# Loading the first tile of a row-maximum kernel by two DMAs, one of 16 partitions and one of 112

## The chip, the cores and the metric

One Trainium2 chip, one core of it. The metric is the device time of a run in microseconds (us). Engines that matter: DVE (VectorE) reduces, SP (SyncE) issues the loads, and 16 DMA engines move the data from HBM into SBUF, the on-chip memory of 128 partitions. Where a number below is called a landing, it is the time from the start of the profiled span to the semaphore event that tells that a DMA is complete.

## The reference

```python
x = np.random.randn(8192, 8192).astype(np.float32)
return np.linalg.norm(x, ord=np.inf, axis=1)      # the largest |x| of each row
```

256 MiB are read once; 32 KB are written.

## The kernel before

48 of the 64 rows that each partition gets are read as 24 bulk tiles, each 128 partitions x 16384 floats (64 KB in each partition, two rows of the input). One `reduce_max` handles a tile. The remaining rows (the tail) are read in smaller and smaller pieces. Three buffers take turns.

```python
x_b = x[:split].rearrange("(a p n b) c -> a n p (b c)", p=P, a=A, n=G, b=B)
...
sbuf = ctx.enter_context(tc.tile_pool(name="sbuf", bufs=BUFS))      # BUFS = 3
...
for a in range(A):
    for n in range(G):
        t = sbuf.tile([P, B * cols + 16], F32, tag="t")
        nc.sync.dma_start(out=t[:, : B * cols], in_=x_b[a, n])
        absmax(r_bulk[:, a, n * B : (n + 1) * B],
               t[:, : B * cols].rearrange("p (b c) -> p b c", b=B))
...                                   # the tail, stores
nc.at_finalize(start_first_load_early)   # moves the first load ahead of the opening barrier
```

Consecutive partitions read addresses 256 KB apart (`n * b * c` floats), and every partition's share of a tile is one contiguous 64 KB run.

Of the kernel before, what the change touches and what calls it, by code (L numbers as in the profile page):

```python
# [1 line left out]
logging.getLogger("concourse").setLevel(logging.ERROR)  # L3

# [1 line left out]

# [4 lines left out]

F32 = mybir.dt.float32
X = mybir.AxisListType.X



TAIL = (
    [[8192]] * 8
    + [[4096, 4096]] * 5
    + [[2048] * 4] * 2  # L20
    + [[2048, 2048, 2048, 1024, 512, 512]]
)


def start_first_load_early(nc):


    sp = mybir.EngineType.SP
    first, *rest = nc.main_func.blocks
    for block in rest:  # L30
        insts = block.instructions
        for i, ins in enumerate(insts):
            if ins.engine == sp and type(ins).__name__ == "InstDMACopy":
                assert not ins.sync_info.on_wait
                moved = insts[i]
                block.instructions = insts[:i] + insts[i + 1 :]
                head = first.instructions
                at = next(k for k, h in enumerate(head) if h.engine == sp)
                first.instructions = head[:at] + [moved] + head[at:]
                return  # L40


@with_exitstack
def kernel(
    ctx: ExitStack,
    tc: tile.TileContext,
    x: bass.AP,
    out: bass.AP,
    G: int = 4,
    B: int = 2,  # L50
    BUFS: int = 3,
):
    nc = tc.nc
    P = nc.NUM_PARTITIONS
    rows, cols = x.shape


    n_tail = len(TAIL)
    assert n_tail % B == 0
    n_bulk_rows = rows // P - n_tail  # L60
    assert n_bulk_rows % (G * B) == 0
    A = n_bulk_rows // (G * B)
    split = n_bulk_rows * P
    x_b = x[:split].rearrange("(a p n b) c -> a n p (b c)", p=P, a=A, n=G, b=B)
    out_b = out[:split].rearrange("(a p n b) -> p a (n b)", p=P, a=A, n=G, b=B)
    x_t = x[split:].rearrange("(p t b) c -> t p (b c)", p=P, b=B)
    out_t = out[split:].rearrange("(p t) -> p t", p=P)

    sbuf = ctx.enter_context(tc.tile_pool(name="sbuf", bufs=BUFS))
    outp = ctx.enter_context(tc.tile_pool(name="outp", bufs=1))  # L70

    k_last = len(TAIL[-1])
    r_bulk = outp.tile([P, A, G * B], F32)
    r_tail = outp.tile([P, n_tail], F32)
    r_fin = outp.tile([P, 1], F32)
    k_max = max(len(r) for r in TAIL[:-1])
    part = outp.tile([P, n_tail - 1, k_max], F32)
    nc.vector.memset(part[:], 0.0)  # L78

    def absmax(o, i):  # L80
        nc.vector.reduce_max(out=o, in_=i, axis=X, apply_absolute_value=True)  # L81

    for a in range(A):
        for n in range(G):
            t = sbuf.tile([P, B * cols + 16], F32, tag="t")
            nc.sync.dma_start(out=t[:, : B * cols], in_=x_b[a, n])
            absmax(
                r_bulk[:, a, n * B : (n + 1) * B],
                t[:, : B * cols].rearrange("p (b c) -> p b c", b=B),
            )  # L90
    nc.scalar.dma_start(out=out_b, in_=r_bulk[:])

    for i in range(0, n_tail, B):
        t = sbuf.tile([P, B * cols + 16], F32, tag="t")
        for j in range(B):
            r = i + j
            at = j * cols
            last = r == n_tail - 1
            for k, w in enumerate(TAIL[r]):
                nc.sync.dma_start(  # L100
                    out=t[:, at : at + w], in_=x_t[i // B][:, at : at + w]
                )
                if last and k == k_last - 1:

                    absmax(r_tail[:, : n_tail - 1], part[:])
                    nc.scalar.dma_start(
                        out=out_t[:, : n_tail - 1], in_=r_tail[:, : n_tail - 1]
                    )
                    absmax(r_fin[:], t[:, at : B * cols + k_last - 1])
                elif last:  # L110
                    absmax(
                        t[:, B * cols + k : B * cols + k + 1], t[:, at : at + w]
                    )
                else:
                    absmax(part[:, r, k : k + 1], t[:, at : at + w])
                at += w
    nc.sync.dma_start(out=out_t[:, n_tail - 1 :], in_=r_fin[:])
    nc.at_finalize(start_first_load_early)


# [1 line left out]
_INS = ['x']  # L122
_OUTS = [((8192,), 'float32')]


# [23 lines left out]
```

## Time and profile before

| | before |
|---|---|
| time, median of 6 runs | 629.2 us |
| span of the profiled run | 627.3 us |
| DMA queue q1, share of 16 engines' time | 99.2% |
| DVE busy | 552.7 us, 88% |
| first bulk reduction starts | 22.03 us |
| distance between later bulk reductions | 19.3 to 19.4 us |

The page of the kernel before: busy times, DMA rate in 40 slices of the span, the load queue, the chain that ended last, and the group of bulk reductions (its last columns are the engine's idle time before them and what ended it).

```profile
DVE 552.7 (88%) x58; POOL 0.2 (0%) x4
GB/s 401 468 401 464 405 460 410 455 414 451 418 451 418 451 418 447 422 447 422 447 422 447 422 447 422 447 422 443 426 420 428 425 433 435 426 429 427 427 425 274
q1 hardware_dynamic: 8208, 268.44, 99.2%
DMA 64%; DVE 30%; another core or an unknown queue 4%; issue 1%; SPq 0%
L81 DVE TENSOR_REDUCE r_bulk<-t 128x2 f32<-128x16384 f32 x24 | 413.3, 17220 | 69.7 <-DMA t<-in_x_dram 69.7
```

The load queue is the limit: it is busy from end to end, while the DVE waits 69.7 us in all before its bulk tiles. The alternation of 401 and 468 in the rate is only that packets are booked at their start: in a finer view of the same trace (its first 23 us in 40 slices) single slices of 0.575 us swing between 0 and 1254 GB/s while the queue is 96.7% busy.

The timeline of the kernel before, its first three bulk reductions (start, duration, engine, line, operation, shapes, and in brackets the idle time before and what ended it):

```profile
22.03 17.22 DVE L81 TENSOR_REDUCE r_bulk<-t 128x2 f32<-128x16384 f32 x1 [21.05 <-DMA t<-in_x_dram]
41.32 17.22 DVE L81 TENSOR_REDUCE r_bulk<-t 128x2 f32<-128x16384 f32 x1 [2.07 <-DMA t<-in_x_dram]
60.67 17.22 DVE L81 TENSOR_REDUCE r_bulk<-t 128x2 f32<-128x16384 f32 x1 [2.14 <-DMA t<-in_x_dram]
```

A reduction takes 17.22 us, a tile's load 19.3 us, so each reduction starts when its tile lands. One level down are the DMA packet records of the trace. Each 64 KB run is one packet. On every one of the 16 engines the packets follow each other without a gap at 2.418 us each (65,536 bytes in 2.418 us are 27.1 GB/s). Eight of them make a tile: 19.34 us.

### The profile page before, as it was taken

How to read it: one execution, taken by the hardware profiler on the slowest of the kernel's cores; microseconds unless marked ns; L12 is line 12 of the kernel's file. 1: busy time of each engine (PE TensorE's matmuls, PEld its weight loads, DVE VectorE, ACT ScalarE, POOL GpSimd, SP SyncE). 2: the span in 40 equal slices, each digit the busy share in tenths (PEclk: the TensorE clock that was granted, in tenths of full speed). 3: DMA queues.
4: the chain of work that ended last, by engine and by line, in shares of the span. 5: the costliest groups of instructions: out<-in, count | busy, mean ns of one | idle time of the engine just before them, and what ended most of it. 6: DMA issues, size and time to landing. Idle time of an engine off the chain costs nothing.

```text
span 627.3 us, 196 instructions
## 1 busy us (share of the span) xinstructions
DVE 552.7 (88%) x58; POOL 0.2 (0%) x4
## 2 busy tenths in 40 slices
DVE  0588988889988889888898888998889999999998
POOL 0000000000000000000000000000000000000000
DMA  9999999999999999999999999999999999999996
GB/s 401 468 401 464 405 460 410 455 414 451 418 451 418 451 418 447 422 447 422 447 422 447 422 447 422 447 422 443 426 420 428 425 433 435 426 429 427 427 425 274
DMA packets 9138, 268.49 MB, mean 428 GB/s; under 512 B 1968, under 2 KB 1968, under 8 KB 2352
## 3 DMA queue, kind: packets, MB, share of 16 engines
q1 hardware_dynamic: 8208, 268.44, 99.2%
q10 hardware_dynamic: 928, 0.03, 0.1%
q14 instruction: 2, 0.02, 0.0%
HBM read 268.44 MB, written 0.03 MB: 428 GB/s over the span
## 4 chain that ended last, share of the span: by engine, by line
DMA 64%; DVE 30%; another core or an unknown queue 4%; issue 1%; SPq 0%
DMA t<-in_x_dram 64%; DVE r_bulk L81 24%; DVE part L81 5%; DVE t L81 1%; SPq L100 0%; DVE r_fin L81 0%
## 5 line engine op out<-in xcount | busy, mean ns | idle before, releaser
L81 DVE TENSOR_REDUCE r_bulk<-t 128x2 f32<-128x16384 f32 x24 | 413.3, 17220 | 69.7 <-DMA t<-in_x_dram 69.7
L81 DVE TENSOR_REDUCE part<-t 128x1 f32<-128x4096 f32 (+2 forms) x26 | 130.0, 5067 | 1.3 <-DMA t<-in_x_dram 1.3
L81 DVE TENSOR_REDUCE t<-t 128x1 f32<-128x2048 f32 (+2 forms) x5 | 8.6, 1746 | 0.3 <-DMA t<-in_x_dram 0.3
L78 DVE MEMSET part<- 128x60 f32 x1 | 0.1, 108 | 0.9 <-PEq L133 0.9
L81 DVE TENSOR_REDUCE r_fin<-t 128x1 f32<-128x517 f32 x1 | 0.7, 691 | 0.0
L81 DVE TENSOR_REDUCE r_tail<-part 128x15 f32<-128x60 f32 x1 | 0.2, 216 | 0.0
L133 POOL MEMSET const-bfloat16-1.0<- 128x1 bf16 x1 | 0.1, 101 | 0.0
L133 POOL MEMSET const-uint8-127<- 128x1 uint8 x1 | 0.1, 101 | 0.0
L133 POOL MEMSET const-float32-0.0<- 128x1 f32 x1 | 0.1, 98 | 0.2 <-issue 0.2
L133 POOL MEMSET const-float32-1.0<- 128x1 f32 x1 | 0.1, 98 | 0.0
## 6 DMA issues: line engine op xcount, KB each, us to landing
t<-in_x_dram SPq DMA_DIRECT2D x8, 4096.0 KB, 37.0
t<-in_x_dram SPq DMA_DIRECT2D x10, 2048.0 KB, 30.4
t<-in_x_dram SPq DMA_DIRECT2D x11, 1024.0 KB, 24.6
t<-in_x_dram SPq DMA_DIRECT2D x1, 512.0 KB, 15.9
t<-in_x_dram SPq DMA_DIRECT2D x2, 256.0 KB, 13.2
t<-in_x_dram SPq DMA_DIRECT2D x24, 40.7
out_dram<-r_bulk ACTq DMA_DIRECT2D x1, 24.0 KB, 57.9
out_dram<-r_tail ACTq DMA_DIRECT2D x1, 7.5 KB, 5.6
```

What stands on the lines that cost most here:

```text
L78: nc.vector.memset(part[:], 0.0)
L81: nc.vector.reduce_max(out=o, in_=i, axis=X, apply_absolute_value=True)
L133: nc = _bacc.Bacc("TRN2", target_bir_lowering=False, num_devices=1)
```

## The change

The first tile is loaded in two parts. The first has 16 partitions, so that each DMA engine has only one descriptor (one contiguous run, one 64 KB packet in the trace); this part is the load that is moved ahead of the opening barrier. The intent is to have all 16 engines at work sooner.

```diff
-            nc.sync.dma_start(out=t[:, : B * cols], in_=x_b[a, n])
+            for lo, hi in ((0, 16), (16, P)) if a == n == 0 else ((0, P),):
+                nc.sync.dma_start(
+                    out=t[lo:hi, : B * cols], in_=x_b[a, n][lo:hi, :]
+                )
```

## The prediction

> **What bounds the kernel now.** The load stream. On the page, queue q1 holds its 16 DMA engines 99.2% of the span and moves 268.44 MB; the DVE is busy 88% and before nearly every bulk reduction it waits about 2.1 us for a DMA (chain of waits, timeline). The trace's packet records show each bulk row as one 65,536-byte packet of 2.418 us, back to back on each of 16 engines (27.1 GB/s each), so a tile of 128 rows costs 8 x 2.418 = 19.34 us, which is the distance between landings (22.00, 41.29, 60.65 us). The DVE needs 17.22 us per tile, so it never sets the pace. The end is start-up, 256 packet times on the engine that lags most, and a tail of about 5 us.
>
> **What the change hopes for.** The first load is issued at 0, its sequencer time is 0.38 us, and the 16 engines take their first packet between 1.02 and 2.05 us; second packets start between 3.89 and 4.75 us. One row per engine should hand all engines work at about 1.0 us. The second part is issued right after the opening barrier (about 0.79 us) and should be queued before a first packet ends. If rows always took 2.418 us, the lagging engine would gain at most 4.75 - 3.89 = 0.86 us; I would say 0.7 us: 628.5 us. The extra issue (0.33 us on SP) is off the path; semaphores shift by one, but every wait keeps its place (instruction orders compared).
>
> **What I think it costs.** Which partitions an engine writes changes. [...] Every load of this trace covers 128 partitions, so it shows nothing of this. [...] The other 112 rows are 7 per engine. [...]the queue has no slack, so nothing is won back. [...]
>
> **On the critical path:** all of it; it delays the first landing from 22.0 to about 38 us and everything after equally.
>
> **Prediction:** 644 us, range 628 to 648. Faster by over 2%: 1%; within 2%: 43%; slower by over 2%: 56%.
>
> **What would show it.** [...] First reduction starting at 36 to 39 us; later landings again 19.34 us apart; the DMA rate low in the page's first slices only; DVE busy time unchanged at 552.7 us.
>
> [...]

The sum came to 644 us: the 629.2 us of the kernel before and about 15 us more, the first landing moving from 22.0 to about 38 us.

## The result

| | before | after |
|---|---|---|
| time, median of 6 runs | 629.2 us (629.04 to 629.8) | 650.55 us (650.19 to 651.07) |
| ratio, 95% interval | | 1.0338 (1.0324 to 1.0351) |
| first landing (both parts) | 22.00 us | 43.32 us |
| DVE busy | 552.7 us | 552.7 us |

The change makes the kernel 21.35 us slower. The ratio is the mean time of the changed kernel's fast runs over that of the other's fast runs of the same rounds, so it is not quite the ratio of the medians.

The same lines of the page, after:

```profile
DVE 552.7 (85%) x58; POOL 0.2 (0%) x4
GB/s 194 251 319 404 441 453 437 412 445 449 404 441 453 429 412 453 445 404 445 449 416 429 453 441 408 445 449 404 441 424 437 431 427 437 419 434 433 422 425 251
q1 hardware_dynamic: 8224, 268.44, 99.0%
DMA 62%; DVE 31%; another core or an unknown queue 4%; issue 1%; SPq 0%; DVEq 0%
L81 DVE TENSOR_REDUCE r_bulk<-t 128x2 f32<-128x16384 f32 x24 | 413.3, 17220 | 90.7 <-DMA t<-in_x_dram 90.7
```

Nearly the whole difference is in the idle time before the bulk tiles, 90.7 - 69.7 = 21.0 of 21.35 us. The rate is low in the first three slices (16.2 us each) and then as before. Note what does not show it: q1 is still "99% busy". A DMA engine that moves data slowly is as busy as one that moves it fast (below: 0.95 busy at 239 GB/s, 0.99 at 431); only the rate tells.

The timeline after:

```profile
43.42 17.22 DVE L81 TENSOR_REDUCE r_bulk<-t 128x2 f32<-128x16384 f32 x1 [42.43 <-DMA t<-in_x_dram]
62.52 17.22 DVE L81 TENSOR_REDUCE r_bulk<-t 128x2 f32<-128x16384 f32 x1 [1.89 <-DMA t<-in_x_dram]
81.87 17.22 DVE L81 TENSOR_REDUCE r_bulk<-t 128x2 f32<-128x16384 f32 x1 [2.13 <-DMA t<-in_x_dram]
```

The first reduction starts 21.39 us later, the second 21.20, the third 21.20; from there on the spacing is as before. The loss is made entirely while the first tile is loading and never won back.

Rates in stretches of the profile after (stretch, its length, busy times of DVE and POOL, clock, DMA share, GB/s): the second part of the first tile, then whole tiles.

```profile
12.00:40.00 28.00, 0.00 (x0) 0.00 (x0) 1.00 0.95 239
44.00:100.00 56.00, 51.08 (x3) 0.00 (x0) 1.00 0.99 431
```

The 112-row DMA moves 239 GB/s where a 128-row DMA moves 431. The packet records of a typical engine make it finer. Durations in us of its first ten packets, before and after (from the trace's packet records; the kept trace does not name the engine, so an engine is followed by joining each packet to the one that starts where it ends):

```
before  2.95  2.42 2.42 2.42 2.42 2.42 2.42 2.42  2.42 2.42
after   8.91  5.29 4.85 3.07 3.61 4.69 4.62 4.59  2.88 2.42
        16 rows|------------- 112 rows ---------|  tile 2
```

A packet's record ends before its data are down: all of the first part's packets end by 10.4 us, but its landings on the 16 engines are at 10.8 to 11.8 us. The loss by part, from landings: 16 rows landing at 11.76 us instead of about 5.07 (22.00 minus seven packets of 2.418), that is 6.7 us; 112 rows in 43.32 - 11.76 = 31.56 us instead of 7 x 2.418 = 16.93, that is 14.6 us. Together 21.3 us.

And the hoped-for gain? The engines take their first packets at 1.02 to 2.05 us before (mean 1.36) and at 1.03 to 1.80 us after (mean 1.35). One descriptor for each engine did not start the average engine sooner in these two profiles; the last one started 0.25 us sooner.

### The profile page after: what moved, and what is told of

It is laid out like the page before. It is cut to its first block, busy times and chain, and to the rows that moved or that the text cites. A ratio compares the mean times of both kernels' runs of the same rounds, so it can differ in the third digit from the quotient of the medians.

```text
span 648.4 us, 198 instructions
## 1 busy us (share of the span) xinstructions
DVE 552.7 (85%) x58; POOL 0.2 (0%) x4
## 4 chain that ended last, share of the span: by engine, by line
DMA 62%; DVE 31%; another core or an unknown queue 4%; issue 1%; SPq 0%; DVEq 0%
DMA t<-in_x_dram 62%; DVE r_bulk L81 25%; DVE part L81 5%; DVE t L81 0%; SPq L104 0%; DVE r_fin L81 0%; DVEq L81 0%
## 5 line engine op out<-in xcount | busy, mean ns | idle before, releaser
L81 DVE TENSOR_REDUCE r_bulk<-t 128x2 f32<-128x16384 f32 x24 | 413.3, 17220 | 90.7 <-DMA t<-in_x_dram 90.7
```

Source lines behind the costliest of these rows:

```text
L81: nc.vector.reduce_max(out=o, in_=i, axis=X, apply_absolute_value=True)
```

## The experiments

The theory: what counts is which partitions of SBUF the engines write at the same time; some sets are written at full speed and others are not. Each run is described by the partitions that it writes. Rivals: a first tile in two DMAs is slow as such; 16 reads at such distances are slow in HBM; the start of the kernel is disturbed. Each edit replaces the load of the kernel before, or the loop of the changed kernel, for the first tile unless said; the diffs are shortened and leave out the condition `a == n == 0` in places. Runs without repeats are one look each; their state is unknown, so only differences of several us and times inside the profile are used. Times at a glance:

| run | first tile loaded as | landing of first part | landing of tile | time |
|---|---|---|---|---|
| before | 128 | - | 22.0 | 629.2 |
| after | 16 + 112 | 11.8 | 43.3 | 650.55 |
| e1_cols | 128 x 2048 columns, 128 x the rest | 4.7 | 21.6 | 629.46 |
| e2_seven | 16 + 7 x 16 | 11.9 | 43.7 | 650.6 |
| e3_spread_to | 8 x 16, writes 8 apart | 7.7 | 43.1 | 650.7 |
| e4_spread_from | 8 x 16, reads 8 apart | 12.7 | 78.1 | 685.6 |
| e5_own_ports | 16, 7 apart from row 11, first | 5.1 | 52.7 | 660.3 |
| e6_one_pair | 16, 7 apart from row 18, first | 7.2 | 44.9 | 652.1 |
| e7_seven_near | as e2, other reads | 11.8 | 43.7 | 650.6 |
| e8_halves | rows 0-63, 64-127 | 23.1 | 43.5 | 650.6 |
| e9_two_pairs | 16, 7 apart from row 17, first | 7.4 | 44.7 | 651.5 |
| e10_middle | rows 32-95, 0-31, 96-127 | 13.4 | 33.5 | 640.7 |
| e11_mid | the split on the ninth tile | - | - | 653.4 |
| e12_eight | 8 rows first, 8 engines | 7.7 | 63.1 | 669.9 |

### e1_cols: two DMAs, but split by columns

```diff
+            cuts = (0, 2048, B * cols) if a == n == 0 else (0, B * cols)
+            for lo, hi in zip(cuts[:-1], cuts[1:]):
+                nc.sync.dma_start(out=t[:, lo:hi], in_=x_b[a, n][:, lo:hi])
```

> The first tile is split into two DMAs by columns (128 x 2048 and 128 x 14336), so both parts touch all 128 partitions. Theory[...]: no loss, 629.2 us within 0.7, first landing at 22.0 us within 0.7. Rival (a first tile in two DMAs, or a small first DMA, costs time by itself): about 650 us as in the changed kernel.

Measured in five rounds: 629.46 us against 629.22, ratio 1.0002 (0.9988 to 1.0016). The first reduction:

```profile
21.75 17.22 DVE L81 TENSOR_REDUCE r_bulk<-t 128x2 f32<-128x16384 f32 x1 [20.77 <-DMA t<-in_x_dram]
```

Two DMAs for a tile, and a small first one (the same 1 MB), cost nothing if both span the 128 partitions: that rival is out. The first tile is ready 0.28 us sooner in this one profile, but the time shows no gain; this was also the version that might have beaten both kernels, and it does not.

### e3_spread_to and e4_spread_from: writes against reads

Eight DMAs of 16 rows load the tile. `near` are 16 neighbouring rows, `apart` are 16 rows 8 apart. One run reads near and writes apart, the other the reverse.

```diff
+            near = [slice(16 * j, 16 * j + 16) for j in range(8)]
+            apart = [slice(j, P, 8) for j in range(8)]
+            for to, of in zip(apart, near):            # e4_spread_from: zip(near, apart)
+                nc.sync.dma_start(out=t[to, : B * cols], in_=x_b[a, n][of, :])
```

> Wrong result on purpose in the first tile (its rows are permuted). Eight DMAs of 16 rows; each reads 16 neighbouring rows of the input, as the 16-row DMA of the change does, and writes partitions 8 apart[...]. [...]the tile lands at 41 us (40 to 44), 648 us (646 to 652). Rival (HBM: 16 reads 256 KB apart are what is slow): [...]landing at about 79 us, 686 us.

> Wrong result on purpose in the first tile. The cross of the run before: each of eight DMAs reads 16 rows that lie 8 apart in the input and writes 16 neighbouring partitions[...]. [...]the tile lands at 79 us (77 to 82), 687 us (684 to 691). Rival (HBM): clearly less than that, 22 to 45 us for the landing.

In both texts the first figures are for the case that the writes set the time.

The results of the first tile's rows are permuted here. The comparison with the reference passed all the same, so it does not notice that permutation; the runs serve for their times alone. Rates while the first tile loads, first e3_spread_to, then e4_spread_from:

```profile
8.00:40.00 32.00, 0.00 (x0) 0.00 (x0) 1.00 0.95 197
```

```profile
12.00:70.00 58.00, 0.00 (x0) 0.00 (x0) 1.00 0.97 108
```

From landing to landing a DMA of 16 rows takes (43.11 - 7.71) / 7 = 5.06 us when it writes partitions 8 apart and (78.14 - 12.68) / 7 = 9.35 us when it writes 16 neighbouring ones. The time goes with the partitions that are written, not with the rows that are read: with the same neighbouring reads, the first DMA landed at 11.76 us in the changed kernel, which writes them to neighbours, and at 7.71 us here, written 8 apart. The 16 packets of 65,536 bytes move at 112 GB/s to neighbours and at 207 GB/s 8 apart; in a whole tile, at 2.418 us a packet, 16 engines move 434 GB/s.

### e2_seven: which rows does the DMA of 112 give to which engine?

```diff
+            rows16 = [slice(0, 16)] + [slice(16 + j, P, 7) for j in range(7)]
+            for r in rows16 if a == n == 0 else [slice(0, P)]:
+                nc.sync.dma_start(out=t[r, : B * cols], in_=x_b[a, n][r, :])
```

> The first 16 rows as in the change; the other 112 as seven DMAs of 16 rows whose partitions are 7 apart (16, 23, ... then 17, 24, ...), one row for each DMA engine. If the DMA of 112 rows gives each engine 7 consecutive partitions, these seven put the same 16 partitions under way at the same time: the tile lands at 43.3 us within 1.5 and the time is 650.5 us within 2.5[...]. If the 112 rows are laid out otherwise, the landing differs by more than 3 us.

Landing 43.71 us against 43.32 and 650.6 us against 650.55, and the packet times match row by row (compare with the line "after" above):

```
e2_seven  8.53  5.14 4.90 2.97 3.83 4.46 4.72 4.51  3.14 2.42
```

So the DMA of 112 rows behaves as one that gives each engine seven neighbouring partitions. In both runs the third and fourth of the seven rows are the short ones (3.07 and 3.61 us, 2.97 and 3.83 us), in e2_seven the DMAs that write partitions 18, 25, ... and 19, 26, ... . Why these two sets are faster than the other five is not shown.

### e5_own_ports, e6_one_pair, e9_two_pairs: the same DMA from row 11, 18 or 17

Each time a DMA of 16 rows that are 7 apart goes first, with nothing before it; only its first row differs: 11, 18 or 17. The rest of the tile follows in whatever DMAs are needed.

```diff
+            parts = [slice(b, b + 106, 7) for b in (11, 17, 12, 13, 14, 15, 16)]   # e5_own_ports
+            parts += [slice(0, 11), slice(123, P)]
+            # e6_one_pair:  b in (18, 16, 17, 19, 20, 21, 22), then slice(0, 16)
+            # e9_two_pairs: b in (17, 16, 18, 19, 20, 21, 22), then slice(0, 16)
+            for r in parts if a == n == 0 else [slice(0, P)]:
+                nc.sync.dma_start(out=t[r, : B * cols], in_=x_b[a, n][r, :])
```

> The first DMA takes 16 rows that lie 7 apart from row 11 on[...]. Then the same from rows 17[...], 12, 13, 14, 15, 16, and the 16 rows left over in two DMAs. [...]the first DMA lands at 4.7 us (4.3 to 5.2), against 11.76 in the changed kernel[...], although it too has one descriptor for each engine and the same distance between the rows that are read as the slow rows of the run seven. Rival (16-row DMAs, or reads 1.75 MB apart, are slow[...]): 6.5 us or later. [...] The time itself says little: 655 to 668 us[...].

> As the run seven, but the DMA[...] (rows 18, 25, ...) goes first, with nothing before it. Expected: 14 engines finish it at 4.1 to 4.9 us and two at 6.5 to 7.2 us[...]. Rival[...]: all 16 at 6.3 us or later. Time about as the changed kernel, 648 to 654 us.

> As the run with one pair, but the DMA[...] (rows 17, 24, ...[...]) goes first, with nothing before it. [...]the 12 engines[...] finish at 6.0 us or later, the four others at about 7 us. Rival (what looked so in the runs before was left over from the DMA before): 12 engines at 4.6 to 5.5 us, four at about 7 us. Time 649 to 654 us.

In the last text the first case is the one in which all engines are held up.

When each of the 16 engines completed that first DMA (semaphore events, us, in order of time, rounded; the engines began at 1.40 to 2.04, 1.40 to 2.05 and 1.42 to 2.35 us):

```
row 11 (e5)  4.64 4.70 4.71 4.71 4.74 4.75 4.78 4.79 4.84 4.87 4.88 4.89 4.89 4.90 5.02 5.12
row 18 (e6)  4.67 4.71 4.77 4.78 4.84 4.85 4.91 4.96 4.97 4.98 4.98 5.01 5.25 5.42 | 6.87 7.17
row 17 (e9)  6.62 6.66 6.71 6.72 6.85 6.85 6.86 6.90 6.93 7.06 7.09 7.20 7.21 7.24 7.25 7.44
```

The profile's own line for that first DMA, its last field the landing, in e6_one_pair and in e9_two_pairs:

```profile
t<-in_x_dram SPq DMA_DIRECT2D x1, 7.2
```

```profile
t<-in_x_dram SPq DMA_DIRECT2D x1, 7.4
```

From row 11, a 16-row DMA with one descriptor per engine is fast: it lands at 5.12 us, against 11.76 us for partitions 0 to 15. From row 18, two engines are late (6.87 and 7.17 us) and the other 14 are not (4.67 to 5.42 us, a little later than the 4.1 to 4.9 expected). The records name no engine, so which two they are is not shown. From row 17, all 16 are late (6.62 to 7.44 us). Nothing ran before these DMAs, so it is not an echo of an earlier one. In e5_own_ports the second DMA is the one from row 17, and there too all 16 engines are late: seven complete it at 8.70 to 9.36 us and nine at 10.09 to 10.52, where one more packet of 2.42 us after 4.64 to 5.12 us would give 7.1 to 7.5 us (an estimate from these figures). The three DMAs have the same number of rows at the same distance, so neither of the two explains the difference: it goes with which 16 they are. That it is the writes and not the reads fits e3_spread_to and e4_spread_from above and e7_seven_near below.

### e7_seven_near: are the held-up engines waiting for reads?

```diff
+            to = [slice(0, 16)] + [slice(16 + j, P, 7) for j in range(7)]
+            near = [slice(16 * j, 16 * j + 16) for j in range(8)]
+            for r, of in zip(to, near):
+                nc.sync.dma_start(out=t[r, : B * cols], in_=x_b[a, n][of, :])
```

> Wrong result on purpose in the first tile. The run seven with other reads: each DMA reads 16 neighbouring rows (256 KB apart instead of 1.75 MB), and writes the same partitions as in seven. If the writes alone set the pace: landing at 43.7 us within 1, 650.6 us within 1.5, row times as in seven. If the reads hold up the engines[...]: landing earlier by 3 us or more (36 to 40).

Landing 43.73 us (e2_seven: 43.71), time 650.6 us (650.6). The eight DMAs land within 0.2 us of those of e2_seven, one by one. Seven times closer reads change nothing. The first reduction in e2_seven, then in e7_seven_near:

```profile
43.83 17.22 DVE L81 TENSOR_REDUCE r_bulk<-t 128x2 f32<-128x16384 f32 x1 [42.85 <-DMA t<-in_x_dram]
```

```profile
43.85 17.22 DVE L81 TENSOR_REDUCE r_bulk<-t 128x2 f32<-128x16384 f32 x1 [42.86 <-DMA t<-in_x_dram]
```

(The first tile's rows are permuted here too.)

### e8_halves and e10_middle: are fewer than 128 rows slow as such?

```diff
-            for lo, hi in ((0, 16), (16, P)) if a == n == 0 else ((0, P),):
+            for lo, hi in ((0, 64), (64, P)) if ...:                   # e8_halves
+            for lo, hi in ((32, 96), (0, 32), (96, P)) if ...:         # e10_middle
```

> The first tile in two DMAs of 64 rows. With 4 neighbouring rows for each engine[...]: 5.1 us a row as measured[...], the first DMA lands at about 22.5 us, the tile at about 43 us, 650.5 us (649 to 652). [...]

> The first tile as three DMAs by rows: 32 to 95, 0 to 31, 96 to 127. With neighbouring rows for each engine, rows 32 to 95 give each of the 16 engines 4 rows[...], so this half tile should land at 11.6 to 12.6 us, where the half tile of rows 0 to 63 landed at 23.1. The two others[...] (5.1 us a row, two rows each): tile landing 32 to 33.5 us, 640 us (638.5 to 642). Rival (a DMA of fewer than 128 rows is slow by itself): first part at about 22 us, 650 us.

Rates while the first 64 rows of e8_halves load (the stretch reaches into the second half), then in e10_middle while rows 32 to 95 load and while the two quarter tiles load:

```profile
8.00:40.00 32.00, 0.00 (x0) 0.00 (x0) 1.00 0.95 197
```

```profile
3.00:11.00 8.00, 0.00 (x0) 0.00 (x0) 1.00 0.91 393
14.00:30.00 16.00, 0.00 (x0) 0.00 (x0) 1.00 0.94 197
```

Sixty-four rows took until 23.1 us as partitions 0 to 63 and until 13.4 us as partitions 32 to 95. In the second case the packets after the first are 2.42 us, as in a full tile. The landing missed the expected 11.6 to 12.6 us. The engines began later in this profile (first packets at 1.43 to 2.41 us, issuing the DMA took 0.65 us instead of 0.38), as they did in e5, e6 and e9; why, and whether that is the whole of the miss, is not known. The number of rows is not the point; which partitions they are is.

### e11_mid: the same split later

```diff
-            ... if a == n == 0 else ((0, P),):
+            ... if (a == 2 and n == 0) else ((0, P),):
```

> The change's split (16 and 112 rows) on the 17th tile instead of the first. [...]the same rows cost the same[...] anywhere in the stream, 21.5 us in all: 650.5 us (648.5 to 652.5). Rival (the loss belongs to the start of the kernel): 629 to 632 us.

The text says the 17th tile; a = 2 and n = 0 is in fact the ninth. Measured 653.4 us, 24.2 us more than before, a little over the expected range. The timeline around it:

```profile
138.20 17.22 DVE L81 TENSOR_REDUCE r_bulk<-t 128x2 f32<-128x16384 f32 x1 [2.13 <-DMA t<-in_x_dram]
159.82 17.22 DVE L81 TENSOR_REDUCE r_bulk<-t 128x2 f32<-128x16384 f32 x1 [4.40 <-DMA t<-in_x_dram]
201.09 17.22 DVE L81 TENSOR_REDUCE r_bulk<-t 128x2 f32<-128x16384 f32 x1 [24.05 <-DMA t<-in_x_dram]
```

The loss does not belong to the start of the kernel. It is larger here, and the tile before is late too: its last rows land at 159.80 us instead of 157.38. That the 16 rows got in its way fits those 2.42 us, but was not tested.

### e12_eight: does it take 16 engines?

```diff
+            parts = [slice(b, b + 22, 3) for b in (0, 1, 2)] + [slice(24, P)]
+            for r in parts if a == n == 0 else [slice(0, P)]:
+                nc.sync.dma_start(out=t[r, : B * cols], in_=x_b[a, n][r, :])
```

> Only eight engines at work: the first DMA takes rows 0, 3, ... 21[...]. [...]all eight land at 6.3 to 7.5 us. If it takes the load of 16 engines to be held up: four land at 4.3 to 5.3 us, four at 6.3 to 7.5 us. The time says nothing here ([...]my guess is 665 to 700 us).

The eight engines complete the first DMA at 6.17, 6.31, 6.32, 6.86, 7.11, 7.12, 7.66 and 7.68 us. None is as early as 5.3 us, so here too all engines of the DMA were held up. It is less clean than e9_two_pairs. The eight were alone only until 4.88 us: by 5.05 us five more engines had begun the DMA of the other 104 rows. An engine that was not held up would have been all but done by then (4.64 to 5.12 us in e5_own_ports, from similar starts), so a load of 16 engines is not what it takes, but how far eight alone are slowed is not shown. Three engines also came in half a microsecond before the rest, the range 6.17 to 7.68 us is slightly wider than expected at both ends, and the packets began at 1.52 to 2.01 us.

## Why the prediction was wrong

- **What bounds the kernel: right.** The load queue; DVE busy time did not move (552.7 us), and the delay of the first landing (21.3 us) reappears in the time (21.35 us) with nothing won back.
- **Cost of the 16-row part: right, shown.** The forecast's term for it was close to the measured 6.7 us. That the partitions written are the cause is shown by the crossed runs (9.35 us for 16 neighbouring partitions, 5.06 for 16 that are 8 apart) and by e5_own_ports (landing at 5.12 us for 16 that are 7 apart from row 11).
- **Start-up gain: not seen.** The prediction took 0.7 us as the gain that was hoped for. First packets start at a mean of 1.35 us against 1.36, and e1_cols gained nothing in time.
- **The failed step: the size of the 112-row term.** The forecast moved the first landing by about 16 us in all. Less the 6.7 us of the first part, that left about 9 us for the 112 rows, and they cost 14.6. The assignment of seven consecutive partitions to an engine was right as far as e2_seven shows it (43.71 us against 43.32). The author's estimate of what follows from it was not: it slowed only some of the engines in each row. What the runs showed in its place: a row can hold up all 16 engines (all land at 6.62 to 7.44 us in e9_two_pairs, against 4.64 to 5.12 in e5_own_ports; e12_eight points the same way), or only two of them (e6_one_pair), though the DMAs differ in their first row alone.
- **Does that account for the missing 5 us?** It is not shown in numbers: the author's repeat of the estimate with engines held up all together rested on the same rule and is cut. What the trace shows is where the time went: the seven packets of the typical engine above add up to 30.72 us, against 7 x 2.418 = 16.93, which is 13.8 of the 14.6 us.
- **Range and chances.** 644 us, 628 to 648, leaned to the right side (slower by over 2% was given 56%), but the measured 650.55 lies 2.55 us above the range.
- **Signs: right in part.** Measured: first-part packets were 7.6 to 9.0 us; in e4_spread_from too the first records are short (7.8 to 9.3 us) and the later ones, also to 16 neighbouring partitions, are 9.4 us. Packets of the second part took 2.8 to 5.8 us and none was as short as 2.42, which is the failed step seen packet by packet. The first reduction started at 43.42 us, not at 36 to 39. Later landings again came every 19.3 us.

What stays open: why the 16 rows from row 17 hold up all engines, those from row 18 two and those from row 11 none. e7_seven_near excludes the distance between the rows read. The runs do not tell where in the path the engines block each other.

## What to carry to other kernels

Before splitting a load by partitions, write down which partitions the engines will write together, row by row, and measure such a set alone. In these runs 16 rows took 9.35 us on 16 neighbouring partitions and 5.06 us on 16 that are 8 apart, where a whole tile takes 2.42 us for its 16 packets at a time; of three sets of 16 that are 7 apart, each written first, one was fast (complete at 5.12 us from the start of the span), one had two late engines (6.87 and 7.17 us) and one had all 16 late (6.62 to 7.44 us). Partitions 32 to 95 landed at 13.4 us, 0 to 63 at 23.1. Other sets were not run, and a rule that would foretell them is not shown. A split by columns keeps all 128 partitions in each DMA and cost nothing here (629.46 us against 629.22). A busy DMA queue says nothing of its speed (0.95 busy at 239 GB/s, 0.99 at 431): look at the rate and at the length of packets.
